# A hybrid encoder layer: the long convolution is woven into the projection in the proportion 400 to 329 instead of 445 to 329

## The chip, the cores and the metric

The kernel runs on one core of a Trainium2 chip. The metric is the device time of one execution in microseconds (us). A core has five engines that run at the same time, each through its own queue of instructions in order: TensorE (PE in the profile: matmuls; PEld is its loading of weights), VectorE (DVE), ScalarE (ACT), GpSimd (POOL) and SyncE (SP), which here issues most of the loads from DRAM. Where an instruction waits for another engine or for a transfer, everything behind it in the same queue waits too.

## The reference, cut to what matters

One encoder layer over 2048 tokens of width 1024. A combined projection feeds two groups of heads; their outputs are joined, projected and added, and cross-attention into 256 memory tokens and an MLP of width 4096 follow.

```python
u = _rms_norm(h, norm_mix_g)
proj = u @ w_in                                   # 1024 -> 1536 + 1024 + 1024 + 16 columns
hy = _short_conv_centred(proj[..., :1536], ...)   # v, x1, x2 of the convolution group
z, g1, g2 = split(hy)
for o, gate in enumerate((g1, g2)):               # "Hyena": two orders
    conv = irfft(rfft(z, 2 * L) * spec[:, o])[:L]
    z = gate * (conv + z * skip[o])
y_hy = _group_rms_norm(z, hy_norm_g, 8)
qk = silu(_short_conv_centred(proj[..., 1536:2560], ...))
y_ml = _mlstm_bidirectional(q, k, v, o_pre, gates)  # a forward and a backward scan over states
mixed = concatenate([y_hy, _group_rms_norm(y_ml, ml_norm_g, 4)])
h = h + mixed @ w_out
h = h + _cross_attention(_rms_norm(h), _rms_norm(mem), wq, wk, wv, wo)
h = h + square(relu(_rms_norm(h) @ ff_w1)) @ ff_w2
return _rms_norm(h, final_norm_g)
```

## The kernel before, in words

All values are fp32. A large product is made of three matmuls of rounded parts (high by high, low by high, high by low: lines L355, L358, L359). So the projection stands in the queue of PE as rows `mm<-xh,wh`, `mm<-xl,wh` and `mm<-xh,wl`.

The work is written as Python generators, each of which emits a stage piece by piece and yields a weight after each piece. The function `program` puts the generators into one order. `weave(a, b, wa, wb)` draws from two of them in turn: it advances `a` as long as `a`'s share of `wa` is not ahead of `b`'s share of `wb`. A scheduler then decides the final order on every engine from that program order and from a simulated timeline; it keeps the dependences.

The stages around the change are these.

- **Projection** (`sweep`, `natural`): first the sweeps of the columns that the convolution needs, later the columns of q, k, v, gates and the output gate. It is part of the chain of generators called `rest`, whose yields sum to about 440.
- **Convolution** (`hyena`): a Fourier transform in factors of 64. For each of two orders: eight "spectrum" blocks that read the signal z (L173 and L186, `hy<-a,f`) and store it to the DRAM tensor zs; an exchange through DRAM; then sixteen "response" steps, which load zs and the filter's blocks fs (L920), compute the filter's response (L956, `mm<-a,dm`), the forward factor (L1030, `hy<-a,dm`) and the factor back (L987, `hy<-b,em`), and store to zg; a second exchange; and eight "inverse" blocks (L173 and L186, `hy<-a,e`), which load zg (L339) and the gate signal (L974). The last order stores its result yh (L1068, POOL). The yields of `hyena` sum to about 335. L173 is the first matmul of a block and L186 the other seven.
- **Gates** (`gates`): the scalars of the mLSTM, with transposes L1093, L1134, L1149 and L1171 on PE.
- **Backward states** (`states`): 15 steps, each of which loads k (L1178) and v (L1184) through SP's queue into two buffers, scales v on POOL (L1196), forms four outer products on PE (L1200, `hy<-va,kn`), adds the old state on DVE (L1206) and stores the new one to DRAM through POOL's queue (L1219, `cbd`).
- **Memory projections** (`memproj`): products of the attention's weights with the memory tokens (L708, `mm<-mt,wm`; L725; L737, `mm<-wm,kt`). They need nothing of the convolution.
- **mLSTM** (`mlstm`): 16 steps; each loads q, k and the backward state (L1258, L1259), makes the scores (L1284), the products with values (L1322) and with the states (L1324), and the forward state's outer products (L1200, `hy<-ve,kn`). The first five yields of the generator are emitted beside `memproj` by `beside_each`; the rest is woven into the output projection and attention, whose first matmuls on PE are the transposes of line L1479.

The proportion in question stands in `program`, which is printed here:

Of the kernel before, what the change touches and what calls it, by code (L numbers as in the profile page):

```python
# [2076 lines left out]
def chain(*gens):  # L2077
    for g in gens:
        yield from g


def weave(a, b, wa, wb, until=False):
    da = db = 0.0
    fa = fb = False
    while not (fa and fb):
        if fb or (not fa and da / wa <= db / wb):
            try:
                da += next(a)
            except StopIteration:
                fa = True  # L2090
        else:
            try:
                db += next(b)
            except StopIteration:
                fb = True
                if until:
                    return


def program(p):  # L2100
    with ExitStack() as ms:
        with ExitStack() as es:
            p.inproj_open(es)
            p.filters_open()
            p.prepq = p.x_first()
            p.pop()
            s = chain(p.sweep(range(4), 0, True, lambda: p.prep_x(1)), p.opened(), p.sweep(range(4), 1, False))
            f = p.filters()
            for _ in range(5):
                next(s)  # L2110
            next(f)
            next(f)
            next(s)
            weave(s, f, 140, 102, True)
            p.gates_open(es)
            n = p.memproj()
            m = p.mlstm(ms)
            with ExitStack() as hs:
                rest = chain(s, p.sweep(range(4, 10), 1, True), p.natural(1, (3, 0, 1, 2), True),
                             p.natural(0, (3,)), among(p.sweep((4, 5, 8, 9), 0, False), p.gates(), 2),  # L2120
                             among(chain(p.natural(0, (0, 1)), p.sweep((6, 7), 0, False),
                                         p.natural(0, (2,), p.prep_mem, 2)), p.states(), 1),
                             )
                weave(rest, p.hyena(hs), 445, 329)
            for _ in chain(p.turned_in(), take(n, 1), beside_each(n, take(m, 5))):
                pass
        with ExitStack() as rs:
            p.ts = rs.enter_context(ExitStack())
            p.tail_open(p.ts)
            with ExitStack() as at:  # L2130
                g = p.attention(at)
                weave(g, m, 440, 112, True)
                ms.close()
                p.ffn_open(rs)
                for _ in g:
                    pass
            p.ffn()


def among(g, h, every):  # L2140
    for i, v in enumerate(g):
        yield v
        if i % every == every - 1:
            next(h, None)
    for _ in h:
        pass


def beside_each(g, h):
    for v in g:  # L2150
        yield v
        yield next(h, 0)
    yield from h


def take(g, n):
    for _ in range(n):
        v = next(g, None)
        if v is None:
            return  # L2160
        yield v
# [31 lines left out]
```

## Time and profile before

| | |
|---|---|
| device time, three runs | 3072.32, 3072.69, 3078.89 us |
| median | 3072.69 us |
| the profiled execution's own time | 3076.22 us |
| its span in the trace | 3074.5 us |
| granted PE clock, mean | 0.987 of full speed |
| PE busy | 2984.5 us (97%) |
| DVE, ACT, POOL busy | 63%, 49%, 41% |

The profile is of one execution. A row of the trace's timeline gives a start, a duration, the engine, the source line and `output<-inputs`, and behind x the number of records; in brackets stands how long the engine was idle before and what released it. A matmul of fp32 data in lines L173 to L1479 leaves two records each; one of the three rounded matmuls leaves one. Matmuls overlap in their pipeline, so the distance between two starts is the price of one and not the duration that stands in the row. In a table of windows, PEclk is the granted clock of PE (1.00 is full speed), and "DMA share" is the mean busy share of the core's 16 transfer engines.

### The profile page before, as it was taken

How to read it: one execution, taken by the hardware profiler on the slowest of the kernel's cores; microseconds unless marked ns; L12 is line 12 of the kernel's file. 1: busy time of each engine (PE TensorE's matmuls, PEld its weight loads, DVE VectorE, ACT ScalarE, POOL GpSimd, SP SyncE). 2: the span in 40 equal slices, each digit the busy share in tenths (PEclk: the TensorE clock that was granted, in tenths of full speed). 3: DMA queues.
4: the chain of work that ended last, by engine and by line, in shares of the span. 5: the costliest groups of instructions: out<-in, count | busy, mean ns of one | idle time of the engine just before them, and what ended most of it. 6: DMA issues, size and time to landing. Idle time of an engine off the chain costs nothing.

```text
span 3074.5 us, 44129 instructions
## 1 busy us (share of the span) xinstructions
PE 2984.5 (97%) x14799; PEld 2369.8 (77%) x14799; DVE 1938.8 (63%) x3442; ACT 1493.0 (49%) x2930; POOL 1259.7 (41%) x1025
## 2 busy tenths in 40 slices
PE   9999999998999988999999999999999999999998
PEld 7666667775678757888887888888888888888876
DVE  7855454657656347867665665557555676566695
ACT  6443455635654236555544455556555543333335
POOL 0112123411344654333133247765566374344653
PEclk9999999999999988999999999999999999999999
DMA  6655687596877965464567466657544565344434
GB/s 219 196 188 171 214 271 219 184 297 200 258 223 249 349 231 192 158 220 131 188 203 259 147 210 216 208 181 243 186 154 151 195 198 171 118 158 120 155 103 164
DMA packets 423643, 607.03 MB, mean 197 GB/s; under 512 B 36846, under 2 KB 229998, under 8 KB 422392
## 3 DMA queue, kind: packets, MB, share of 16 engines
q1 hardware_dynamic: 395972, 525.42, 53.3%
q0 software_dynamic: 18992, 62.96, 5.6%
q10 hardware_dynamic: 8452, 15.83, 1.4%
q8 instruction: 117, 1.92, 0.3%
q14 instruction: 110, 0.90, 0.1%
HBM read 401.67 MB, written 202.41 MB: 196 GB/s over the span
## 4 chain that ended last, share of the span: by engine, by line
PE 58%; DVE 2%; DMA 1%; issue 1%; ACT 0%; POOL 0%; SPq 0%; DVEq 0%; ACTq 0%; POOLq 0%
PE mm L355 12%; PE mm L359 12%; PE mm L358 12%; PE hy L355 6%; PE hy L359 6%; PE hy L358 6%; PE hy L1322 1%; PE hy L1324 1%; DVE bl L1693 0%; PE hy L1284 0%; PE hy L1479 0%; PE hy L1596 0%; DVE acc L1991 0%; PE hy L1200 0%; DVE acc L2028 0%
## 5 line engine op out<-in xcount | busy, mean ns | idle before, releaser
L1692 ACT CAST ah<-w 128x512 fp32r<-128x512 f32 x284 | 176.7, 623 | 304.0 <-PE hy L358 157.8
L1693 DVE TENSOR_TENSOR bl<-wr,bh 128x512 fp32r<-128x512 f32 x213 | 235.5, 1110 | 131.1 <-ACT bh L1692 131.0
L366 DVE TENSOR_TENSOR wl<-wn,wh 128x512 fp32r<-128x512 f32 (+1 forms) x296 | 216.6, 775 | 94.3 <-ACT wh L366 94.3
L355 PE MATMUL mm<-xh,wh 128*128 128x512 f32 x640 | 263.3, 413 | 3.7 <-ACT wh L366 1.2
L358 PE MATMUL mm<-xl,wh 128*128 128x512 f32 x640 | 254.1, 397 | 4.5 <-DVE xl L366 4.4
L1692 ACT CAST bh<-wr 128x512 fp32r<-128x512 f32 x232 | 143.4, 621 | 229.0 <-PE mm L359 177.5
L359 PE MATMUL mm<-xh,wl 128*128 128x512 f32 x640 | 253.7, 397 | 0.0
L1693 DVE TENSOR_TENSOR al<-w,ah 128x512 fp32r<-128x512 f32 x236 | 213.6, 905 | 55.7 <-ACT ah L1692 55.6
L359 PE MATMUL mm<-bh,al 128*128 128x512 f32 x576 | 223.7, 391 | 4.0 <-DVE al L1693 4.0
L355 PE MATMUL mm<-bh,ah 128*128 128x512 f32 x576 | 225.8, 392 | 0.1
L358 PE MATMUL mm<-bl,ah 128*128 128x512 f32 x576 | 224.9, 390 | 0.0
L366 ACT CAST wh<-wn 128x512 fp32r<-128x512 f32 (+1 forms) x296 | 164.4, 620 | 105.8 <-PE mm L359 51.0
L358 PE MATMUL mm<-act,wh 128*128 128x512 f32 x512 | 202.0, 394 | 0.0
L355 PE MATMUL mm<-act,wh 128*128 128x512 f32 x512 | 199.4, 396 | 2.0 <-ACT wh L366 1.9
L359 PE MATMUL mm<-act,wl 128*128 128x512 f32 x512 | 199.9, 392 | 0.0
L355 PE MATMUL hy<-bh,ah 128*128 128x512 f32 x448 | 175.2, 391 | 0.0
L358 PE MATMUL hy<-bl,ah 128*128 128x512 f32 x448 | 174.6, 390 | 0.0
L359 PE MATMUL hy<-bh,al 128*128 128x512 f32 x448 | 174.4, 390 | 0.0
L331 POOL TENSOR_TENSOR b<-b 128x512 f32<-128x512 f32 x32 | 48.1, 1505 | 294.6 <-DVE b L330 275.2
L355 PEld LDWEIGHTS mm<-xh,wh 128*128 128x128 f32 x640 | 120.5, 188 | 53.1 <-issue 19.4
L358 PEld LDWEIGHTS mm<-xl,wh 128*128 128x128 f32 x640 | 120.6, 188 | 49.2 <-issue 18.6
L355 PE MATMUL mm<-wh,xh 128*128 128x256 f32 (+1 forms) x512 | 154.7, 302 | 0.0
(396 smaller groups left out, 8262.9 us busy)
## 6 DMA issues: line engine op xcount, KB each, us to landing
wr<-hc SPq DMA_DIRECT2D x224, 256.0 KB
w<-in_ff_w_dram SPq DMA_DIRECT2D x172, 256.0 KB
hc<-wn SPq DMA_DIRECT2D x128, 256.0 KB
wn<-in_w_in_dram SPq DMA_DIRECT2D x100, 256.0 KB
hc<-q SPq DMA_DIRECT2D x96, 256.0 KB
fs<-a SPq DMA_DIRECT2D x32, 512.0 KB
zs<-a POOLq DMA_DIRECT2D x32, 512.0 KB, 6.0
a<-fs SPq DMA_DIRECT2D x64, 256.0 KB
```

The costliest lines, as they stand in the source:

```text
L331: nc.gpsimd.tensor_tensor(b, f, b, ALU.subtract)
L355: first = mm(ps, lh, rh, start=start, stop=False)
L358: mm(ps, lh, rl, start=False, stop=False)
L359: self.last = mm(ps, ll, rh, start=False, stop=stop)
L366: both = (self.nc.scalar.copy(hi, src), self.nc.vector.tensor_tensor(lo, src, hi.bitcast(F32), ALU.subtract))
L1322: nc.tensor.matmul(dst, nm[:, h], va[:, h], start=True, stop=state is None)
L1324: nc.tensor.matmul(dst, rows_[d, 1][:, h], state[:, h], start=False, stop=True)
L1692: self.nc.scalar.copy(hi, src)
L1693: eng.tensor_tensor(lo, src, hi.bitcast(F32), ALU.subtract)
```

## The change

One number changes. The weight of `rest` in the weave with `hyena` becomes 400; that of `hyena` stays.

```diff
--- before.py
+++ after.py
@@ -2121,7 +2121,7 @@
                              among(chain(p.natural(0, (0, 1)), p.sweep((6, 7), 0, False),
                                          p.natural(0, (2,), p.prep_mem, 2)), p.states(), 1),
                              )
-                weave(rest, p.hyena(hs), 445, 329)
+                weave(rest, p.hyena(hs), 400, 329)
             for _ in chain(p.turned_in(), take(n, 1), beside_each(n, take(m, 5))):
                 pass
```

`weave` itself is the same in both:

```python
def weave(a, b, wa, wb, until=False):
    ...
    while not (fa and fb):
        if fb or (not fa and da / wa <= db / wb):
            ...  # da += next(a); at its end fa = True
        else:
            ...  # db += next(b); at its end fb = True
```

In weights the convolution's last piece was emitted when 335 x 445 / 329 = 453 of `rest` would have been emitted, that is at its end; now it is emitted at 335 x 400 / 329 = 407 of about 440. Instructions are neither added nor removed. What moves lies between the first spectrum block and the fourth mLSTM step; from there on PE's order is the same. In the scheduled order the last of the eight inverse blocks stood among the memory projections behind six others; two of the eight stood within the projection. Now five stand within the projection and three among the memory projections. Of the 15 state steps nine stood within the projection and six among the memory projections; now it is six and nine.

The end of the memory projections and the first mLSTM steps on PE (L708 and L737 belong to `memproj`, L1284 to L1324 and `ve,kn` to the mLSTM, `va,kn` to the backward states). Before:

```order
L708 MATMUL mm<-mt,wm 128x256 x3
L737 MATMUL mm<-wm,kt 128x512 x8
L708 MATMUL mm<-mt,wm 128x256 x6
L173 MATMUL hy<-a,e_2743 32x512
L186 MATMUL hy<-a,e_2743 32x512 x7
L708 MATMUL mm<-mt,wm 128x256 x10
L737 MATMUL mm<-wm,kt 128x512 x10
L1284 MATMUL hy<-qn,kk_t 128x128 x8
L737 MATMUL mm<-wm,kt 128x512 x6
L1322 MATMUL hy<-va,rw 128x129 x5
L1324 MATMUL hy<-cbn,rw 128x129
```

Now:

```order
L1200 MATMUL hy<-va,kn 128x129 x4
L1284 MATMUL hy<-qn,kk_t 128x128 x8
L737 MATMUL mm<-wm,kt 128x512 x2
L708 MATMUL mm<-mt,wm 128x256 x8
L1322 MATMUL hy<-va,rw 128x129 x6
L708 MATMUL mm<-mt,wm 128x256 x3
L1324 MATMUL hy<-cbn,rw 128x129
L1322 MATMUL hy<-va,rw 128x129
L1324 MATMUL hy<-cbn,rw 128x129 x2
L1322 MATMUL hy<-va,rw 128x129
L1324 MATMUL hy<-cbn,rw 128x129
L708 MATMUL mm<-mt,wm 128x256 x4
```

The last state step (`va,kn`) now stands right ahead of the first scores (L1284), and matmuls of the memory projections stand between those of mLSTM step 0; of step 1 the same holds in the rows that follow. Before, all but six of them stood ahead of the first L1322.

PE where the first order's last response step begins after the second order's exchange of z through DRAM (the projection's L355 to L359, a transpose of projected columns L825, and the first forward factor L1030, which reads the loaded zs). Before, the last rows ahead of it, behind the last spectrum block and 19 other projection matmuls:

```order
L358 MATMUL mm<-xl,wh 128x512
L359 MATMUL mm<-xh,wl 128x512
L355 MATMUL mm<-xh,wh 128x512
L358 MATMUL mm<-xl,wh 128x512
L359 MATMUL mm<-xh,wl 128x512
L825 MATMUL mm<-ident,cv 128x128 x4
L1030 MATMUL hy<-a,dm 128x512 x2
```

Now, from the last spectrum block on:

```order
L186 MATMUL hy<-a,f_104 64x512 x7
L355 MATMUL mm<-xh,wh 128x512
L358 MATMUL mm<-xl,wh 128x512
L359 MATMUL mm<-xh,wl 128x512
L355 MATMUL mm<-xh,wh 128x512
L358 MATMUL mm<-xl,wh 128x512
L359 MATMUL mm<-xh,wl 128x512
L355 MATMUL mm<-xh,wh 128x512
L358 MATMUL mm<-xl,wh 128x512
L359 MATMUL mm<-xh,wl 128x512
L956 MATMUL mm<-a,dm 128x512 x2
L1030 MATMUL hy<-a,dm 128x512 x2
```

Between the last spectrum block of that order and the first L1030 there now stand nine projection matmuls and two of the filter's response (L956) instead of 24 projection matmuls with transposes. The transposes of the gates (L1093 to L1172), which stood among the inverse and spectrum blocks of the first order, now stand behind that place.

SP's queue at the last loads of the backward states (L1178 k, L1184 v, L415 the weights of `memproj`, L1258 and L1259 the loads of the first mLSTM steps). Before:

```order
L415 DMA wm<-in_xa_wo_dram 128x1024 x2
L1178 DMA kn<-kn 128x512
L1184 DMA va<-vd 128x4x128
L415 DMA wm<-in_xa_wv_dram 128x4x256 x2
L415 DMA wm<-in_xa_wo_dram 128x1024 x3
L1258 DMA cbn<-cbd 128x516 x2
L415 DMA wm<-in_xa_wo_dram 128x1024
```

Now:

```order
L1178 DMA kn<-kn 128x512
L1184 DMA va<-vd 128x4x128
L415 DMA wm<-in_xa_wv_dram 128x4x256 x2
L415 DMA wm<-in_xa_wo_dram 128x1024 x2
L1178 DMA kn<-kn 128x512
L1184 DMA va<-vd 128x4x128
L415 DMA wm<-in_xa_wo_dram 128x1024 x2
L1259 DMA qn<-qt 128x4x128
L1259 DMA kk_t<-kt 128x4x128
L1259 DMA qn<-qt 128x4x128
L1259 DMA kk_t<-kt 128x4x128
L1258 DMA cbn<-cbd 128x516 x2
```

Between the two last pairs of state loads stand four loads of weights. The load of the backward state for mLSTM step 0 (`cbn<-cbd`), which needs the store of the last state, stood behind five loads of weights; now it stands behind two of weights and four of q and k.

## The prediction

> **What bounds the kernel now.** The page first: TensorE is busy nearly throughout.
>
> ```profile
> span 3074.5 us, 44129 instructions
> ...
> PE 2984.5 (97%) x14799; PEld 2369.8 (77%) x14799; DVE 1938.8 (63%) x3442; ACT 1493.0 (49%) x2930; POOL 1259.7 (41%) x1025
> ```
>
> The change adds and removes no instruction, so only what PE loses can move: about 90 us of idling and the stretches at a lower granted clock. The order differs only between the first spectrum block and the fourth mLSTM step, so I read a table of windows over that part.
>
> ```profile
> core 0: us, PE busy (x) PEld busy (x) DVE busy (x) ACT busy (x) POOL busy (x), PEclk, DMA share, GB/s
> 345.00:430.00 85.00, 80.66 (x459) 56.14 (x458) 42.91 (x68) 45.85 (x72) 11.39 (x18) 1.00 0.85 291
> ...
> 636.00:745.00 109.00, 96.26 (x611) 63.95 (x603) 63.86 (x190) 40.19 (x72) 13.68 (x23) 0.95 0.81 266
> 745.00:985.00 240.00, 237.13 (x1216) 175.88 (x1215) 151.09 (x254) 140.25 (x237) 91.81 (x101) 1.00 0.75 232
> 985.00:1122.00 137.00, 131.75 (x636) 97.74 (x636) 55.73 (x168) 34.35 (x75) 84.68 (x102) 0.98 0.92 309
> 1122.00:1182.00 60.00, 39.19 (x224) 35.99 (x223) 40.72 (x141) 33.29 (x129) 28.01 (x26) 0.74 0.61 195
> ```
>
> They are: the first spectrum blocks; the first order's inverse blocks and the exchange; the second responses beside the projection; the memory projections; the first mLSTM steps. The last one stands out: 20.8 us of its 60 are idle, and the clock is 0.74. The second loses 12.7 us of idling and, at 0.95, some 5 us of clock. The other three idle 4.3, 2.9 and 5.3 us. So the prize is the tail, and what can be lost lies in the rows whose DMA share is high: 0.85, 0.81 and 0.92.
>
> **The change part by part.** *The mLSTM steps at the end.* Before, only six L737 were left when the first L1322 came. The timeline of PE:
>
> ```profile
> 1102.05 4.58 PE L708 MATMUL mm<-mt,wm 128*128 128x256 f32 x20
> 1106.47 8.75 PE L737 MATMUL mm<-wm,kt 128*128 128x512 f32 x20
> 1115.05 1.95 PE L1284 MATMUL hy<-qn,kk_t 128*128 128x128 f32 x16
> 1116.84 5.32 PE L737 MATMUL mm<-wm,kt 128*128 128x512 f32 x12
> 1121.99 1.28 PE L1322 MATMUL hy<-va,rw 128*128 128x129 f32 x10
> 1123.11 0.39 PE L1324 MATMUL hy<-cbn,rw 128*128 128x129 f32 x2
> ...
> 1167.57 0.66 PE L1479 MATMUL hy<-ident,wn 128*128 128x128 f32 x4 [0.70 <-DVE cf L1206]
> ```
>
> From the first L1322 to the first L1479 it is 45.6 us. In it stand, by the order, 88 matmuls of the steps; ten records, or five matmuls, take 1123.11 - 1121.99 = 1.12 us, 0.224 each, so the work is 19.7 us and 25.9 are lost. The longest wait:
>
> ```profile
> PE hy L1322 <- DVE den L1330: 4.6, 1, 4.6
> ```
>
> A step is a chain through PE and DVE, and nothing fills it. After the change 16 L737 and 8 L708 stand among steps 0 and 1. An L737 costs two records at (1115.05 - 1106.47)/20 = 0.429 us, an L708 two at (1106.47 - 1102.05)/20 = 0.221: 13.7 + 3.5 = 17.2 us of work that stood ahead of the steps and now lies beside them. It can win no more than these two steps lose. That is read from where step 2's scores begin:
>
> ```profile
> 1139.83 1.16 PE L1284 MATMUL hy<-qn,kk_t 128*128 128x128 f32 x8 [0.93 <-DVE cf L1206]
> ```
>
> Steps 0 and 1 take 1139.83 - 1121.99 = 17.8 us and hold 40 of the 88 matmuls, 9.0 us: 8.9 lost, the wait of 4.6 among it. The other 17.0 are lost in steps 2 and 3, which stay bare; there the clock has a share.
>
> ```profile
> 1142.00:1152.00 10.00, 5.84 (x24) 5.30 (x24) 6.50 (x28) 2.12 (x12) 1.26 (x1) 0.51 0.29 79
> 1152.00:1162.00 10.00, 7.17 (x31) 6.88 (x32) 7.13 (x26) 6.24 (x26) 7.31 (x7) 0.50 0.39 133
> ```
>
> The clock is halved for 20 us in which PE shows 13.0 us of busy work, so up to 6.5 us are the clock's. It fell behind the wait of 4.6, which will have cover; but two bare steps can bring it down by themselves, so I count half, 3. Together -12. Least gain -6 (the chain's end, not PE, sets the time of step 1: a third of the 8.9 stays). Most -22: the 8.9, the 6.5, and the waits of steps 2 and 3 shortened because the loads and row copies that they need have run ahead.
>
> *The first spectrum blocks*, 20 projection matmuls earlier and two of them back to back. In the densest windows of 50 us the transfers are already full (the third row is a piece of the first):
>
> ```profile
> 350.00:400.00 50.00, 46.28 (x265) 32.85 (x265) 20.89 (x33) 23.01 (x37) 6.56 (x12) 1.00 1.00 348
> 1000.00:1050.00 50.00, 47.69 (x252) 38.67 (x251) 17.95 (x53) 11.05 (x25) 30.96 (x36) 0.97 1.04 357
> 390.00:400.00 10.00, 10.00 (x45) 8.26 (x45) 1.30 (x3) 1.56 (x3) 1.06 (x2) 1.00 1.03 382
> ```
>
> A weave that is 445/400 = 1.11 tighter asks for the same bytes beside 11% less work. In 50 us that is 5.5 us less cover, which idles if the transfers cannot go faster than 348 GB/s; ten us at 382, which is 1.10 of it, say that they can. So 0 to +5. I take +2.5. The Trainium skill ("DMA: Bandwidth & Descriptors", Where 436 GB/s comes from) gives about 358 GB/s as a core's limit towards DRAM: by it hardly anything of the 11% is to be had, and this term would be +5 and the sum -6. The trace agrees over 50 us and not over ten.
>
> *The first order's inverse blocks and the exchange.* The gates leave this place and the responses come up. Waits, and the clock where they fell:
>
> ```profile
> PE hy L1030 <- DMA a<-zs: 3.6, 1, 3.6
> PE hy L1134 <- DVE ends L1129: 2.7, 1, 2.7
> ```
>
> ```profile
> 710.00:720.00 10.00, 5.57 (x23) 2.05 (x24) 9.77 (x26) 3.54 (x6) 0.53 (x1) 0.66 0.39 122
> ```
>
> With the gates goes L1134's wait, 2.7 us, and the clock's loss of 0.34 x 10 = 3.4 us, if they find cover where they now stand (if not, both come back there). Against it stands the exchange:
>
> ```profile
> 729.47 0.48 PE L355 MATMUL mm<-xh,wh 128*128 128x512 f32 x1
> ...
> 733.00 0.39 PE L355 MATMUL mm<-xh,wh 128*128 128x512 f32 x1
> ...
> 739.70 3.49 PE L1030 MATMUL hy<-a,dm 128*128 128x512 f32 x4 [3.62 <-DMA a<-zs]
> ```
>
> The first row stands right behind the last spectrum block, and the first L1030 starts at 739.7: a chain of 10.2 us through ScalarE, the store to zs and the load. Fifteen projection matmuls lie between the first two rows, so nine cost 9 x 3.53/15 = 2.1 us; two L956 have the shape of an L737, four records of 0.429. That is 3.8 us of cover now. So L1030 waits 6.4 instead of 3.6: +2.8, and a longer stretch at a lower clock behind it (the 5 us from 740 on stand at 0.72), +1.7. An inverse, a spectrum and an inverse block stand back to back once, for +1. Sum -2.7 - 3.4 + 2.8 + 1.7 + 1 = -0.6; I take -0.5. From -7 (the exchange no slower) to +8 (the gates' waits return, and the transfers cost here too what the first blocks cost at most).
>
> *The state steps among the memory projections*, nine instead of six. One step's loads, SP's issues and POOL's scaling:
>
> ```profile
> 1075.54 0.53 SPq L1184 DMA_DIRECT2D va<-vd  x1
> 1076.44 4.76 SPq L415 DMA_DIRECT2D wm<-in_xa_wv_dram  x2
> 1081.30 10.70 SPq L415 DMA_DIRECT2D wm<-in_xa_wo_dram  x3
> 1093.11 0.80 SPq L1258 DMA_DIRECT2D cbn<-cbd  x2
> ```
>
> ```profile
> 1085.24 1.03 POOL L1196 TENSOR_TENSOR va<-va,cols 128x516 f32<-128x516 f32 x1 [10.91 <-DMA va<-vd]
> 1089.03 0.57 POOL L1219 DMA_DIRECT2D cbd<-cb  x1 [0.60 <-issue]
> ```
>
> From the load's issue to the scaling's start it is 9.7 us; with 1.0 of scaling and four L1200 (0.9) a buffer returns after 11.6. There are two buffers, so two steps must hold 11.6 us of work. From the counts in the changed order (13 L708, 8 L737 and 4 L1200 make 5.7 + 6.9 + 0.9 = 13.5; a neighbouring pair 12 to 16) they do, by some 2 us; and this stage, at a DMA share of 0.92, loses three of six inverse blocks with their loads to the roomier one before it, at 0.75. I take +0.5, between -4 (most of this stage's 5.3 us of idling goes) and +10 (four pairs, each 2.5 late).
>
> *The first state's way through DRAM.* The load of cbn for step 0 needs the last store. Store to load issue took 1093.11 - 1089.03 = 4.1 us, and the store came 3.8 after the scaling began, about 2 after L1200. With a landing of the load between another 4.1 and the 9.7 us of the va load (not shown itself) the chain is 10.2 to 15.8. Between the last L1200 and the first L1324 there now stand 8 L1284, 2 L737, 11 L708 and 6 L1322: 1.8 + 1.7 + 4.9 + 1.3 = 9.7 us. So +0.5 to +6; I take +1, since the loads of weights are ending there.
>
> *Sum:* 2.5 - 0.5 + 0.5 + 1 - 12 = -8.5. Against the profiled execution of 3076.2 (1.7 of it outside its span) this is 3067.7. That execution stands 3.5 above the median of 3072.7, which would go to 3064.2, say 3064.
>
> **The rivals.** *The clock stays up* (a larger gain): with cover in steps 0 and 1 no wait there is long, and the 20 us at half clock vanish. For it: they begin behind one wait of 4.6 us. Against it: steps 2 and 3 are bare and were at 0.50 themselves, with PE over half busy. It gives -22 in the tail, and with the other terms at 0 3051. The Trainium skill ("TensorE: Matmul & The Clock Gate", Part 1) has the clock halve after an idle window of some 3.4 us and return after a busy one; by it there would be no half clock without such a wait. The trace agrees behind the wait of 4.6, not with the 20 us that follow. Chance 0.14.
>
> *No change*: the convolution is limited by its transfers and takes its stages' time whatever stands beside it; what is won at the end is paid at the start (+5), in the exchange (+5) and by the states (+4), while the tail gives the 12: +2, or 3074, and with the tail at its own forecast and the stages at half of that, 3068. For it: shares of 1.00 to 1.04. Against it: only windows of 50 us are full; their stages stand at 0.81 to 0.92. I give it 3072. Also here belongs that the change does not do what it says: three of eight inverse blocks still stand behind the projection. Chance 0.29.
>
> *Slower: the state steps become the bound.* Their loads stand in SP's queue behind loads of weights, which wait for PE to free their buffers; one issue took 4.8 us and three took 10.7. If a load no longer runs ahead, a step costs 11.6 us in a row. Eight intervals hold, by the order, some 78 us of work; 8 x 11.6 = 93, so +15, and with cbn's late store +6 and the start +2.5 against -12: about +11, 3084. It decides from 8 x 10.9 us on, where it eats the sum's 9. For it: the last four steps stand within 28 us of work. Against it: two buffers, and the longest wait for POOL before was short:
>
> ```profile
> PE hy L1200 <- POOL va L1196: 2.9, 1, 2.9
> ```
>
> Chance 0.17. The forecast itself has the remaining 0.40.
>
> **How the numbers follow.** A measurement of this kernel tells about 0.2%, 6 us, from no change. The forecast at -8.5 is faster in three quarters of its weight: 0.30, and 0.10 the same. The larger gain adds 0.14 faster. No change: 0.05 faster, 0.20 same, 0.04 slower. The slower one: 0.02 same, 0.15 slower. Together 0.49, 0.32, 0.19. The range reaches from the larger gain, 3051, to 3081, into the slower one; the forecast's own is 3056 to 3071.
>
> **What would show it.** Right: from the first L1322 to the first L1479 the time grows by less than 6 us (17.2 - 12) although 17 us of memory projections now stand in it; L1030 waits about 6 us for zs; L1134 waits for nothing; at most three L1200 wait over 2 us for L1196. Wrong: PE idles more than 8 us between 345 and 430, or the half clock in the mLSTM steps is as long as before, or L1324 waits long for cbn.

## The result and the profile after

The changed kernel takes 3092.85 us (median of four executions, 3087.25 to 3096.83) against 3072.51 before (3071.01 to 3078.89). The ratio is 1.0061, with a 95% interval of 1.0038 to 1.0084: slower by 0.4 to 0.8%, where I forecast 3064 and a range up to 3081.

The profiled execution took 3087.25 us, the fastest of the four. So the traces account for 11 us of the 20; for the other 9, before's profiled execution (3076.22) lay 3.7 us above its median and this one 5.6 below. The page of after:

```profile
span 3085.5 us, 44149 instructions
...
PE 2983.5 (97%) x14799; PEld 2367.2 (77%) x14799; DVE 1951.7 (63%) x3442; ACT 1493.0 (48%) x2930; POOL 1258.9 (41%) x1025
```

PE does the same work; what grew is what it loses. To compare two orders I sum, along each kernel's own order on PE, the price of every matmul at full clock (0.227 us for one of the projection of 512 columns, 0.858 for an L737, and so on, each from the distance of its starts in the trace of before). That is the *work* ahead of an instruction; its start time less its work is what PE has lost until then, by waiting or by a low clock. The stages below are cut at the same work in both: 320, 400, 500, 750, 960, 1072 and 1100 us. The windows of before at these cuts, and then of after (columns as in the prediction's table of windows):

```profile
336.60:422.70 86.10, 81.76 (x469) 57.66 (x468) 41.88 (x65) 42.91 (x67) 9.97 (x17) 1.00 0.81 280
422.70:527.50 104.80, 100.46 (x503) 72.12 (x502) 58.74 (x93) 66.00 (x116) 36.48 (x39) 0.98 0.75 233
527.50:793.70 266.20, 253.01 (x1458) 181.75 (x1457) 169.82 (x354) 140.85 (x247) 71.55 (x84) 0.98 0.73 232
793.70:1004.80 211.10, 208.68 (x1153) 160.99 (x1152) 127.99 (x240) 114.47 (x202) 86.29 (x97) 1.00 0.77 240
1004.80:1127.70 122.90, 116.90 (x558) 85.37 (x557) 46.94 (x142) 28.72 (x65) 77.80 (x93) 0.97 0.90 307
1127.70:1187.00 59.30, 39.23 (x212) 35.68 (x211) 39.60 (x135) 32.28 (x125) 26.19 (x24) 0.74 0.59 191
```

```profile
336.70:432.00 95.30, 86.00 (x451) 57.27 (x450) 45.71 (x71) 46.71 (x74) 13.34 (x20) 0.95 0.79 263
432.00:540.50 108.50, 101.44 (x462) 69.34 (x461) 65.54 (x105) 72.30 (x127) 39.07 (x42) 0.98 0.81 245
540.50:823.10 282.60, 259.08 (x1474) 184.00 (x1473) 170.71 (x348) 143.27 (x253) 71.81 (x87) 0.96 0.70 216
823.10:1038.20 215.10, 209.11 (x1213) 165.51 (x1212) 134.12 (x262) 101.31 (x179) 96.89 (x107) 0.99 0.78 244
1038.20:1154.90 116.70, 112.86 (x564) 88.28 (x563) 39.54 (x131) 36.47 (x97) 62.39 (x75) 1.00 0.88 297
1154.90:1199.90 45.00, 32.89 (x186) 27.94 (x185) 31.46 (x113) 24.99 (x94) 22.45 (x22) 0.81 0.70 217
```

Each row's length is the time that the stage took. The last stage went from 59.3 to 45.0 us and the memory projections from 122.9 to 116.7: the gain at the end is there, 20.5 us. It is overpaid: the first spectrum blocks went from 86.1 to 95.3, the first responses from 104.8 to 108.5, the stage with the inverse blocks, the exchange and the gates from 266.2 to 282.6, and the second responses from 211.1 to 215.1, together 33.3 us. The DMA share in the worst stage fell, from 0.73 to 0.70: it is not the transfers as a whole that ran out.

What PE waited for in the first stage, before:

```profile
PE hy L173 <- DMA a<-hy: 1.5, 1, 1.5
PE hy L173 <- ACT a L998: 1.2, 1, 1.2
PE hy L173 <- ACT a L311: 1.1, 1, 1.1
```

And after:

```profile
PE hy L173 <- ACT a L998: 3.7, 1, 3.7
PE hy L173 <- DMA a<-hy: 2.9, 1, 2.9
PE hy L173 <- ACT a L311: 2.7, 1, 2.7
```

Three waits of about 3 us, and the clock of the stage falls from 1.00 to 0.95 with them, which is 95.3 x 0.05 = 4.8 us more. Two of the three are not for a transfer: L998 is ScalarE's copy of the spectrum block before, L311 its copy of the filter's spectrum. In the stage from 527 to 793 before, five smaller waits stand behind the two that the prediction shows (L1030 3.6, L1134 2.7):

```profile
PE hy L173 <- DMA a<-zg: 2.4, 1, 2.4
PE hy L173 <- issue: 1.8, 1, 1.8
PE hy L173 <- DVE a L1051: 1.3, 1, 1.3
PE mm L825 <- ACT P L788: 0.8, 1, 0.8
PE mm L845 <- DVE a L960: 0.5, 1, 0.5
```

And after, from 540 to 823:

```profile
PE mm L956 <- DVE a L960: 7.3, 1, 7.3
PE hy L1030 <- DMA a<-zs: 4.4, 1, 4.4
PE hy L173 <- DMA a<-zg: 2.9, 2, 2.7
PE hy L173 <- DVE a L1051: 2.6, 2, 1.4
PE hy L173 <- ACT a L998: 1.8, 2, 1.0
PE mm L956 <- ACT P L788: 1.7, 1, 1.7
PE mm L956 <- DMA a<-fs: 1.6, 1, 1.6
```

By the windows this stage idles 13.2 us before and 23.5 after; that is 10.3 of its 16.4 us, and the lower clock, 0.96 instead of 0.98, is about the rest. The longest wait is new. The responses' copies L959 and L960 stand in VectorE's queue behind the gates' work (L1114, L1115), which now lies between them, and behind the convolution of projected columns (L798, L799). VectorE in that stretch of the timeline:

```profile
761.40 1.30 DVE L798 SCALAR_TENSOR_TENSOR cv<-P,par,cv 128x1040 f32<-128x1040 f32 x1
762.62 1.37 DVE L1114 TENSOR_TENSOR pad<-pad 64x128 f32<-64x128 f32 x1
...
769.70 0.29 DVE L1115 TENSOR_TENSOR pad<-pad 64x128 f32<-64x128 f32 x1
...
771.10 0.69 DVE L959 COPY a<-mm 64x512 f32<-64x512 f32 x1
771.80 0.69 DVE L960 COPY a<-mm 64x512 f32<-64x512 f32 x1
```

The end, on PE: memory projections now stand between the products of steps 0 and 1, and from the first L1322 to the first L1479 it is 47.9 us, 2.3 more than before, with 17 us of work moved in.

```profile
1133.34 1.50 PE L1322 MATMUL hy<-va,rw 128*128 128x129 f32 x12
...
1140.37 5.31 PE L737 MATMUL mm<-wm,kt 128*128 128x512 f32 x12
...
1181.21 0.66 PE L1479 MATMUL hy<-ident,wn 128*128 128x128 f32 x4 [0.70 <-DVE cf L1206]
```

### The profile page after: what moved, and what is told of

Its sections match the earlier page's. It is cut to its first block, busy times and chain, and to the rows that moved or that the text cites. A ratio compares the mean times of both kernels' runs of the same rounds, so it can differ in the third digit from the quotient of the medians.

```text
span 3085.5 us, 44149 instructions
## 1 busy us (share of the span) xinstructions
PE 2983.5 (97%) x14799; PEld 2367.2 (77%) x14799; DVE 1951.7 (63%) x3442; ACT 1493.0 (48%) x2930; POOL 1258.9 (41%) x1025
## 4 chain that ended last, share of the span: by engine, by line
PE 80%; DMA 6%; DVE 5%; issue 5%; ACT 2%; POOL 1%; SPq 1%; DVEq 0%; POOLq 0%; ACTq 0%
PE mm L355 17%; PE mm L358 17%; PE mm L359 17%; PE hy L359 6%; PE hy L358 6%; PE hy L355 6%; PE mm L956 2%; PE hy L173 2%; PE hy L1030 1%; PE hy L987 1%; PE hy L1322 1%; DMA va<-vd 1%; PE hy L1324 1%; PE hy L1200 1%; PE mm L737 1%
## 5 line engine op out<-in xcount | busy, mean ns | idle before, releaser
L1693 DVE TENSOR_TENSOR bl<-wr,bh 128x512 fp32r<-128x512 f32 x213 | 242.4, 1143 | 125.6 <-ACT bh L1692 125.3
L355 PE MATMUL mm<-xh,wh 128*128 128x512 f32 x640 | 269.1, 422 | 4.5 <-ACT wh L366 1.6
L359 PE MATMUL mm<-xh,wl 128*128 128x512 f32 x640 | 254.3, 398 | 0.0
L359 PE MATMUL mm<-bh,al 128*128 128x512 f32 x576 | 224.1, 392 | 3.8 <-DVE al L1693 3.8
L355 PE MATMUL mm<-bh,ah 128*128 128x512 f32 x576 | 226.2, 393 | 0.6 <-DVE acc L1854 0.5
L355 PE MATMUL mm<-act,wh 128*128 128x512 f32 x512 | 199.2, 395 | 1.3 <-ACT wh L366 1.3
L359 PE MATMUL mm<-act,wl 128*128 128x512 f32 x512 | 199.5, 392 | 0.0
L355 PE MATMUL hy<-bh,ah 128*128 128x512 f32 x448 | 175.2, 391 | 0.0
L359 PE MATMUL hy<-bh,al 128*128 128x512 f32 x448 | 174.4, 390 | 0.0
L355 PEld LDWEIGHTS mm<-xh,wh 128*128 128x128 f32 x640 | 121.6, 190 | 59.1 <-issue 24.2
L355 PE MATMUL mm<-wh,xh 128*128 128x256 f32 (+1 forms) x512 | 155.0, 303 | 0.4 <-DVE st L203 0.4
```

The costliest lines, as they stand in the source:

```text
L355: first = mm(ps, lh, rh, start=start, stop=False)
L359: self.last = mm(ps, ll, rh, start=False, stop=stop)
L1693: eng.tensor_tensor(lo, src, hi.bitcast(F32), ALU.subtract)
```

## The experiments

Theory A: each stage's loss follows from how little other work stands beside the convolution's chain at that place; the losses of the stages add up; so the change lost in the first half more than its second half won. Rivals were that the convolution's earlier end itself costs the time (B), that a loss is taken up again later (C), that the gates' VectorE work is what costs (D), and others named where they stand.

Most kernels set the pace stage by stage. `weave` takes a table of pairs, convolution's weight and weight of `rest`, and draws along straight lines between them:

```diff
-def weave(a, b, wa, wb, until=False):
+def weave(a, b, wa, wb, until=False, knots=None):
...
+    xs, ys = zip(*(knots or ((0, 0), (wb, wa))))
...
-        if fb or (not fa and da / wa <= db / wb):
+        if fb or (not fa and da <= (np.interp(db, xs, ys) if knots else db * wa / wb)):
```

The convolution's own weights are 52 at the first spectrum block, 85.6 behind the eighth, 168.2 at the first inverse block, 216.2 behind the second order's spectrum blocks, 298.8 at the last inverse blocks and 334.8 at the end. The proportion before is a straight line to (334.8, 452.9), that of the change one to (334.8, 407.1).

What the profiles lost in each stage, in us, by the work at its ends (the first of the stages has the first spectrum blocks, the third the exchange, the fifth the memory projections, the sixth the mLSTM steps):

| kernel | 320-400 | -500 | -750 | -960 | -1072 | -1100 | sum | last inverse block at |
|---|---|---|---|---|---|---|---|---|
| before | 6.1 | 4.8 | 16.2 | 1.1 | 10.9 | 31.3 | 70.4 | 1047 |
| the change | 15.3 | 8.5 | 32.6 | 5.1 | 4.7 | 17.0 | 83.2 | 987 |
| the change, second profile | 13.9 | 6.6 | 35.5 | 5.1 | 6.5 | 18.3 | 85.9 | 987 |
| e1, second half alone | 6.7 | 5.2 | 26.0 | 9.0 | 1.3 | 22.7 | 70.9 | 994 |
| e2, first half alone | 16.6 | 8.4 | 27.5 | 8.1 | 12.8 | 24.1 | 97.5 | 1034 |
| e3, first blocks alone | 18.0 | 2.1 | 15.1 | 2.1 | 8.5 | 30.8 | 76.6 | 1047 |
| e4, gates earlier | 19.2 | 6.4 | 37.9 | 6.4 | 4.5 | 19.7 | 94.1 | 987 |
| e5, 425/329 | 6.5 | 6.1 | 25.0 | 7.2 | 4.9 | 26.2 | 75.9 | 1018 |
| e6, last inverse blocks alone | 6.4 | 7.1 | 17.4 | 1.7 | 8.6 | 23.4 | 64.6 | 1023 |
| e7, exchange spread | 16.0 | 2.4 | 13.6 | 0.8 | 10.9 | 29.1 | 72.8 | 1047 |
| e8, paced by stage | 8.9 | 2.0 | 12.1 | 7.5 | 15.2 | 25.6 | 71.3 | 1018 |
| e9, paced, second try | 6.6 | 7.6 | 16.5 | 7.9 | 16.0 | 17.1 | 71.7 | 1008 |
| e10, last inverse closer | 6.1 | 5.0 | 15.6 | 1.5 | 7.0 | 24.7 | 59.9 | 1002 |
| e11, gates later | 18.9 | 9.7 | 30.8 | 6.3 | 7.8 | 19.5 | 93.0 | 987 |

The two profiles of the change, one order, differ by up to 2.9 us in a stage, so differences of that size between single profiles tell nothing. Behind 1100 us of work PE's order is the same in all kernels (but for the first few us), and yet that part took from 1881 to 1889 us; so a profile's time can differ from another's by some us for which no stage of the table accounts.

**e1: the second half alone.**

```diff
-                weave(rest, p.hyena(hs), 445, 329)
+                weave(rest, p.hyena(hs), 445, 329, knots=((0, 0), (216.2, 292.4), (334.8, 407.1)))
```

> The proportion is 445/329 up to the end of the second order's spectrum blocks and then tighter, so that the convolution ends where the change ends it (407 of the projection's weight). First half as before, second half as the change has it. Theory A (the change's loss lies in the first spectrum blocks and around the exchange, its gain in the memory projections and the mLSTM steps, and the stages add up): those two stages gain 15 to 19 us as in the change's trace, the tighter second responses cost 2 to 5; about 3058, faster by 0.3 to 0.6%. Rival B (pulling the convolution's end forward itself costs the time, in transfers moved beside the projection): 3075 to 3090.

Measured: 3076.29 us against 3074.13, ratio 1.001 (1.0001 to 1.002). The time lies in rival B's range, the profile agrees with each theory in part: the last two stages gained 18.2 us as theory A says (42.2 to 24.0), but the tighter second responses lost 7.9 more, and the stage with the exchange 9.8 more, though its spectrum blocks end as before. The second responses begin 5 us of work nearer behind them, and the two waits of that place grew from 3.6 and 2.7 us to:

```profile
PE hy L1030 <- DMA a<-zs: 7.6, 1, 7.6
PE hy L1134 <- DVE ends L1129: 4.4, 1, 4.4
```

So "the second half alone" is not free of the first: whoever wants the convolution's end earlier by a straight pace squeezes the exchange's last link with it.

**e2: the first half alone.**

```diff
-                weave(rest, p.hyena(hs), 445, 329)
+                weave(rest, p.hyena(hs), 445, 329, knots=((0, 0), (216.2, 262.9), (334.8, 452.8)))
```

> The proportion is 400/329 up to the end of the second order's spectrum blocks and then looser, so that the convolution ends where it ended before. First half as in the change, second half as before. Theory A: the first spectrum blocks lose 12 us and the exchange with the gates behind it some 15, nothing is gained at the end: 3095 to 3102. Rival B (the loss lies in the second half): within 6 us of before, 3068 to 3078.

Measured: 3092.18, ratio 1.0063 (1.0043 to 1.0082). The whole loss of the change is here, with only 5.3 of the 20.5 us that its last two stages gained: its profile, 3098.42 us, lost 60.6 us up to 960 against 28.2 before. So rival B does not explain the change: the convolution ends at nearly the same place as before, and the time is lost all the same. (e10 below pulls the end forward and is faster.) The least that theory A allowed was 3 us too high. One part speaks against theory A: the second responses have more projection beside them here than before (1.60 of its weight to 1 of the convolution's, not 1.35), and that stage lost 8.1 us instead of 1.1. Why stays open.

**e3: only the first eight blocks.**

```diff
-                weave(rest, p.hyena(hs), 445, 329)
+                weave(rest, p.hyena(hs), 445, 329, knots=((0, 0), (85.6, 104.1), (168.2, 227.5), (334.8, 452.8)))
```

> Only the eight first spectrum blocks stand as in the change; from the first inverse block on the order is that of before. Theory A: the three waits there (2.7, 2.9 and 3.7 us, each followed by 3.4 us at half clock) cost 10 to 12 us in all, and nothing later gives them back: 3083 to 3085. Rival C (the lost time is taken up later, since a stage behind it waits for transfers that then come in time): 3072 to 3077.

Measured: 3078.07, ratio 1.0015 (1.0005 to 1.0025), or 4.6 us. The profile shows both to be half right: the first stage loses 11.9 us more, by the three waits of the change,

```profile
PE hy L173 <- DMA a<-hy: 5.4, 1, 5.4
PE hy L173 <- ACT a L998: 3.7, 1, 3.7
PE hy L173 <- ACT a L311: 2.7, 1, 2.7
```

and the stages behind it lose 5.7 less, 2.7 of it in the first responses, which have more work beside them here. In the change they have not, and lose 3.7 more instead. That the looser pace is what gives the time back is not shown: in e7 the first responses are tighter than before and lose as little (2.4).

**e4 and e11: the gates earlier, the gates later.** Both are the change (400) with

```diff
-    among(p.sweep((4, 5, 8, 9), 0, False), p.gates(), 2)
+    among(p.sweep((4, 5, 8, 9), 0, False), p.gates(), 1)   # e4; 3 in e11
```

> The change with the gates drawn one to each piece of the projection's sweep instead of one to two, so that their scalar work stands beside the exchange again and not in the second responses. Rival D (the gates' VectorE work among the second responses is the largest loss: a wait of 7.3 us and 10 us at half clock): 3078 to 3083, some 10 below the change. Theory A (the exchange and the gates cost about the same wherever they meet; before, the gates cost two waits and 6.8 us of half clock there): 3086 to 3094, within 6 us of the change.

> The change with the gates drawn one to three pieces of the projection, so that their VectorE work stands some 35 us of work further into the second responses. Rival D (the gates' work beside the exchange is what the change's stage from 500 to 750 loses): the wait of 7.3 us and its 10 us of half clock go from there and return later only in part; 3078 to 3086. Theory A (the squeezed exchange itself is the larger part, the gates cost what they cost wherever the responses stand): 3086 to 3094.

Measured: e4 3100.43, ratio 1.0085 (1.0069 to 1.0101); e11 3090.81, ratio 1.0067 (1.0052 to 1.0083). In e4 the waits of that stage changed their names and the stage lost more, 37.9 us:

```profile
PE mm L355 <- ACT a L962: 4.8, 1, 4.8
PE mm L956 <- DMA a<-fs: 4.7, 2, 3.1
PE hy L987 <- ACT we L1167: 4.5, 1, 4.5
PE hy L173 <- DMA a<-zg: 4.3, 2, 3.5
```

and in e11, with the gates drawn later (their first transpose at 713 us of work, not 680, the last at 797, not 751), the wait of 7.3 us is gone, and the stage still lost 30.8 us against 32.6 and 35.5 in the change's two profiles. Rival D falls: the wait of 7.3 us behind the gates is where the squeeze shows in the change, not what most of the loss comes from. Theory A's bounds held for e11; e4 was worse than they allowed.

**e5: half the way.**

```diff
-                weave(rest, p.hyena(hs), 445, 329)
+                weave(rest, p.hyena(hs), 425, 329)
```

> The proportion 425/329: the same change, a bit under half as far. Theory A (each stage's loss comes from how little projection work stands beside the convolution's chain; a wait above some 2 us costs a further stretch at half clock): the loss in the first half is about half of the change's 25 us, the gain at the end more than half of its 20, since the convolution ends 20 us of work earlier, before the last state: 3070 to 3080. Rival E (the loss grows in proportion): 3082.

Measured: 3075.57, ratio 1.0007 (0.9996 to 1.0019): no difference that can be told. The first blocks lose no more than before (6.5 against 6.1), the stage with the exchange about as much more as in e1 (25.0). The loss does not grow in proportion: the first blocks lose nothing yet, the second responses (7.2) already no less than in the change (5.1).

**e6 and e10: only the last inverse blocks.**

```diff
-                weave(rest, p.hyena(hs), 445, 329)
+                weave(rest, p.hyena(hs), 445, 329, knots=((0, 0), (298.8, 404.2), (334.8, 425.0)))  # e6; 412.0 in e10
```

All that stands ahead of them is as before.

> All as before up to the second order's responses; only its eight inverse blocks are drawn closer (the convolution ends at 425 of the projection's weight). Theory A: first half and responses lose what they lose before; the gain is the end of the convolution's tail over the mLSTM steps: 3062 to 3068. Rival F (the mLSTM steps wait for the backward states, whose last step moves from 1034 to 1058 us of work here, and not for the convolution): no gain, 3072 to 3080.

> As e6, with the last inverse blocks drawn closer still (last one at 1002 us of work, against 1023 in e6 and 1047 before). Theory A: the second half loses 26 to 28 instead of 32; 3062 to 3066. Rival F (here the last backward state, at 1056, sets the mLSTM steps, or the dense inverse blocks wait for their loads): 3068 to 3078, no better than e6.

Measured: e6 3068.14, ratio 0.9984 (0.9972 to 0.9996); e10 3065.51 against 3070.61, ratio 0.9983 (0.9973 to 0.9993). Both are faster than before, by some 5 us, and than the change by more than 20; theory A's range held for e10 and missed e6 by 0.1 us. The stages of e10:

```profile
335.70:421.80 86.10, 81.80 (x469) 57.76 (x468) 41.87 (x65) 42.95 (x67) 9.97 (x17) 1.00 0.79 280
421.80:526.80 105.00, 100.56 (x503) 71.67 (x502) 58.71 (x93) 66.04 (x116) 36.45 (x39) 0.98 0.75 232
526.80:792.40 265.60, 252.54 (x1458) 181.68 (x1457) 169.68 (x354) 140.82 (x247) 71.51 (x83) 0.99 0.73 233
792.40:1003.90 211.50, 208.26 (x1151) 159.23 (x1151) 132.60 (x247) 112.95 (x198) 87.82 (x100) 1.00 0.78 238
1003.90:1122.90 119.00, 116.19 (x558) 86.27 (x557) 45.75 (x138) 31.91 (x74) 76.23 (x91) 0.99 0.94 327
1122.90:1175.60 52.70, 35.48 (x210) 32.09 (x210) 36.82 (x133) 30.38 (x120) 25.55 (x24) 0.81 0.60 194
```

The first four take the times of before to within 0.6 us, the last two 10.5 us less. Rival F falls: the last backward state stands later here than before (at 1056 and 1058 us of work, against 1034), and the steps behind it still lose less. The profile of e10, 3060.34 us, is the fastest of its executions; the gain to count on is the interval's, 2 to 8 us.

**e7, e8, e9: other paces.** e7 spreads the exchange alone; e8 sets the pace of every stage; e9 keeps the first blocks of before and tries again.

```diff
-                weave(rest, p.hyena(hs), 445, 329)
+                weave(rest, p.hyena(hs), 445, 329, knots=(
+                # e7: (0, 0), (85.6, 115.8), (168.2, 216.6), (216.2, 292.4), (334.8, 452.8)
+                # e8: (0, 0), (52, 70.3), (85.6, 120.7), (168.2, 221.5), (216.2, 298.3), (298.8, 401.5), (334.8, 430.0)
+                # e9: (0, 0), (94.2, 127.4), (168.2, 223.0), (216.2, 298.3), (298.8, 408.0), (334.8, 428.0)
+                ))
```

> Only the first order's inverse blocks and the second spectrum blocks are spread over more projection work (76 of weight instead of 65), at the cost of a tighter first response stage, which loses nothing in any trace so far. All else as before. Theory A: that stage's 16.5 us of loss fall by 4 to 8: 3066 to 3070. Rival G (its loss lies in the chain from the last spectrum block to the first forward factor, whose cover is unchanged, and in the gates): 3072 to 3077.

> The pace is set stage by stage: first spectrum blocks and the exchange looser than before, first and second responses tighter, last inverse blocks tighter, end at 430 of weight. Theory A: start -2, exchange -5, second responses +2, end -6 to -10: 3060 to 3066, faster than both. Rival H (the order of before lies where all these trade against each other): 3070 to 3078.

> The first spectrum blocks as before, the exchange spread as in e8, the second responses at before's pace, and the last inverse blocks drawn close, so that the last one stands some 40 us of work earlier than before (1008 against 1047). Theory A (a stage's loss depends on the work beside it, and the loss behind 960 us of work on where the convolution ends: 42 us at 1047, 32 at 1023, 24 at 994): first half 27 to 32 (before 28), second half 26 to 30 (before 42): 3058 to 3066. Rival H (all trades against each other): 3070 to 3076.

Measured: e7 3071.63, ratio 0.9995 (0.9981 to 1.0008); e8 3074.18, ratio 1.0001 (0.9989 to 1.0012); e9 3071.65, ratio 1.0004 (0.9993 to 1.0015). Three misses of theory A's numbers; e8 and e9 lie in rival H's ranges, e7 between A's and G's. In e7 and e8 the spread exchange lost 2.6 and 4.1 us less, the first of which two profiles can't tell from nothing; in e9, spread as in e8, it lost as much as before (16.5). In e7 the tighter first responses brought the first L1030 too near to the first blocks (a wait of 4.2 us for zs), and the first stage lost 9.9 more. In e8 and e9 it was the second responses (6.4 and 6.8 more) and the memory projections (4.3 and 5.1 more). By the table this is rival H's case: each place that I loosened tightened another that had stood just loose enough. Of the places moved, only the last inverse blocks, which have no exchange behind them, cost nothing elsewhere.

**e12: the change itself, once more.**

> The changed kernel itself, a second profile: the first one is of its fastest execution, 5.6 us below its median. Theory A: most of these 5.6 us lie in the first spectrum blocks, where the wait for the z loads was 2.9 us in that profile and 5.4 to 7.7 in four kernels with the same order there; so a wait of 5 to 8 us there, a stage loss of 17 to 20 (15.3 in the first profile), and a time of 3090 to 3096. Rival: that wait is 3 us again and the difference lies in the exchange or at the end.

Measured: 3089.04 us, one execution. The rival was nearer: the wait for the z loads was 1.6 us this time, 2.9 in the first profile and 5.4 to 7.7 in four other kernels with the same order at that place; the stage lost 13.9, and the 2 us more lay in the exchange. The waits for L311 (2.7) and L998 (3.7) are the same to 0.1 us in all six profiles with that order. What separates the two profiles, 3087 and 3089, from the change's median of 3093 was in neither, and stays open.

## Why the prediction was wrong, step by step

- *The end.* The mLSTM steps: right, in kind and about in size. I took -12; the last stage lost 14.3 less (31.3 to 17.0), and between the first L1322 and the first L1479 10 us at half clock are left of 24. One reading was wrong: behind the wait of 4.6 us, which ended at 1135.2, the clock was halved for only 3.4 us; the 20 us at half clock began at 1142.2, around waits of 0.9 and 2.3 us. The memory projections: the wrong sign. I took +0.5 for nine state steps and +1 for the load of cbn; they lost 6.2 less, since they idle 2.2 us less by the windows and their clock went from 0.97 to 1.00. The slower rival in which the state steps become the bound had the right sign for the wrong reason: L1200 waited once, for 2.1 us.
- *The first spectrum blocks.* Mis-sized: +2.5, with +5 as its bound, measured +9.2 (and +7.8 in the second profile). The bound was wrong in kind. I priced the squeeze as transfers at their limit. But two of the three waits end with a copy on ScalarE, and I counted no clock there: 4.8 us of the stage are the clock's. I had priced just that, a stretch of low clock behind a wait, for the exchange, and left it out here. PE idled 9.3 us, which the prediction had named as a sign of being wrong (over 8). The rule of the Trainium skill that I set beside this term ("DMA: Bandwidth & Descriptors", Where 436 GB/s comes from) gave +5 and bears on one of the three waits at most; the stage's DMA share fell from 0.81 to 0.79.
- *The exchange.* The step that failed: -0.5, with +8 as its bound, measured +16.4. The part that I looked at came better than forecast: L1030 waited 4.4 us, not 6.4, and L1134 for nothing. What I booked as gone with the gates, 6.1 us of a wait and its clock, was no gain: a wait of 7.3 us stood on L956 instead, and with the gates earlier (e4) or later (e11) the stage lost 37.9 and 30.8. And I priced two waits, where a whole stage was squeezed: the smaller waits went from five of 0.5 to 2.4 us to more and longer ones (five of 1.6 to 2.9 in the list of after), and the stage's clock from 0.98 to 0.96. The tighter first half alone made this stage lose 11.3 more (e2), the tighter second half alone 9.8 (e1), by the responses that come up behind the exchange. Which link makes up how much of it stays open.
- *The responses.* No term at all. The first lost 3.7 and the second 4.0 more. They wait for almost nothing before (4.3 and 2.4 us of idling in their windows), and I read a stage without waits as a stage with room. Where they were tighter, in e1, e5, e8 and e9, the second ones lost 6 to 8 us more. How tight they are does not set the amount alone: the change, tighter than e5, lost 4.0 more, and e2, where they are looser than before, 7.0 more.
- *The sum.* -20.5 at the end and +33.3 ahead of it give +12.8 where I had -8.5; the stages behind 1100 us of work gave back some 2. Of the 20 us between the medians the profiles show 11, so how the rest is shared among these terms no trace shows.
- *The rivals.* "No change" came nearest in kind: what is won at the end is paid ahead of it. It put that down to transfers and priced it at less than half. With the prices measured it would have been a slower case.

## What to carry to other kernels

A proportion that weaves two streams moves every place where they touch, not only the end that one looks at: take the loss of each stage, not of the one with the largest idle time, and ask of each how far its chain is from being bare. A stage that shows no waits may stand at the edge; its slack is seen only by moving it. When the gain sits at one place, change the pace at that place alone: here drawing the last eight blocks together gave some 5 us, and the weave that brings their end 15 us of work further forward by its whole pace cost 20.

## What the runs showed of the hardware

The price of a wait is more than the wait. In the change's first stage 9.3 us of waits came with a granted clock of 0.95 over 95 us, 4.8 us more: behind each of the three waits, of 2.7, 2.9 and 3.7 us, stand 3.4 us at a clock of 0.50. Before, with waits of 1.1 to 1.5 us at the same places, the stage's clock was 1.00. And a wait for ScalarE's copy repeated to 0.1 us from kernel to kernel (3.7 us in six profiles), while a wait for a transfer at the same place, with the same order, took anything from 1.6 to 7.7 us.
